# A chain of two transformer blocks on one NeuronCore: instruction order from the detailed timing model, stacked transposes one tile later, V's first step moved, ten products added at the start

## The chip, the cores and the metric

One core of a Trainium2 chip runs the whole program in one launch. The metric is the device time of that launch in microseconds (us), as the median of several executions. One further execution is recorded by the hardware profiler; all rows of the trace come from that one.

## What is computed

Input x has 512 tokens of 1024 features. It goes through two blocks; every intermediate is 32-bit.

```python
def first_block(x, ...):                      # DEPTH = 2
    for i in range(2):
        mix = dsa_mixer(h) if i == 0 else gla_mixer(h)
        h = layer_norm(ALPHA * h + mix)
        h = layer_norm(ALPHA * h + squared_relu_mlp(h, w_up, w_down))
# dsa_mixer: q (16 heads x 64), k, v (4 heads x 64), and an indexer (8 heads x 64) whose scores
#   choose the 128 best keys of each query; softmax attention over the chosen keys; @ w_o
# gla_mixer: gated linear attention with 4 heads; @ w_o
def second_block(x, c, ...):
    mod = silu(c) @ w_ada + b_ada             # six rows: shifts, scales, gates
    h = modulate(rms_norm(x), ...); proj = h @ w_in
    y_attn = axial_gqa_attention(...)         # 8 query heads, 2 key heads, 64 wide, full softmax
    y_mem  = bidirectional_mlstm(...)         # 4 heads x 128
    x = x + g1 * (concat(y_attn, y_mem) @ w_out)
    x = x + g2 * ffn(modulate(rms_norm(x), ...))
    return rms_norm(x)
```

## The kernel before

**Tiling.** Tokens lie in four tiles of 128 rows. The activations stand a second time transposed, split into a high and a low part (`xT_hi`, `xT_lo`) that TensorE multiplies in its faster 32-bit form; each weight piece is split in the same way (`wh`, `wl`, `Net.wsplit`: ScalarE copies the high part at L88, VectorE subtracts at L85). A product of two such operands is three products, high x high, high x low, low x high, all issued by the helper `mm` at L77. That is why most rows of TensorE are on L77.

**Order.** The code is written with a tile scheduler. It simulates the program, and at every moment gives each engine the ready instruction of highest priority, which normally is the one that the program wrote first. The result is a fixed instruction stream per engine; on the chip each engine works its stream in that order and waits where an operand isn't ready. `Net.urgent` gives weight loads and weight splits a priority ahead of everything else. Before the change the simulation behind this is the library's default one.

**Two hand-written lists** say which step the program writes when. `ORDER_A` is for the first block's attention: S is a score tile of the indexer, B the search for the best keys of a tile (16 rounds on VectorE, L533 and L534, closed by L535), V a step of V's projection (two tiles of tokens), Q0 and Q1 steps of the query projections, A an attention tile (tile, head group), O an output projection tile, X the reload of x. `ORDER_2` does the same for the second block (VM, AQ and KV are projections, C the convolution's, A attention, M and N the mLSTM).

**Projections.** `proj_steps` (L146) multiplies tile by tile and calls `evac(t, ps)` when a tile's sum stands in PSUM. For the heads that go into attention, `evac` rotates the tile on VectorE, splits it into high and low parts stacked side by side (`hst`, `kst`, `qst`), and calls `transpose_stack` (L398), which transposes them on TensorE (L405) and copies them out on ScalarE (L407). The buffers `qst` and `kst` of the second block are single.

**Start.** `load_x` (L1412) loads the four token tiles in halves, in the order 1, 2, 3, 0, and between them the first weight chunk; it writes the split of these weights first and the transposes of the tokens (`transpose_half`, L298) after it.

**Big stages.** `w_sums` and `proj_seven` do seven half-size products in place of eight in the MLPs: 44 groups of them, each closed by additions on VectorE (L290 to L294).

Of the kernel before, what the change touches and what calls it, by code (L numbers as in the profile page):

```python
# [11 lines left out]
F32R = mybir.dt.float32r  # L12
# [5 lines left out]

ORDER_A = "S2 V S3 V S1 Q0 B1 Q0 A00 A10 Q1 A11 B2 A20 A01 B3 Q1 A30 X A21 O O O A31 O".split()


ORDER_2 = [x.split() for x in ("VM VM AQ AQ KV W KV C",
# [2 lines left out]
P = 128  # L27
# [10 lines left out]
class Net:  # L38
    def __init__(self, ctx, tc, ins, out):
        self.tc, self.nc, self.ins, self.out = tc, tc.nc, ins, out  # L40
        nc = self.nc
        self.cp = ctx.enter_context(tc.tile_pool(name="cp", bufs=1))
        self.wp = ctx.enter_context(tc.tile_pool(name="wp", bufs=2))
        self.sp = ctx.enter_context(tc.tile_pool(name="sp", bufs=4))
        self.pp = ctx.enter_context(tc.tile_pool(name="pp", bufs=2, space=PSUM))
        self.new_xt()
        self.xh = self.cp.tile([P, KB, S], F32R, name="xT_hi")
        self.xl = self.cp.tile([P, KB, S], F32R, name="xT_lo")
        self.ident = self.cp.tile([P, P], F32, name="ident")
        make_identity(nc, self.ident)  # L50
        self.identr = self.cp.tile([P, P], F32R, name="identr")
        nc.vector.tensor_copy(self.identr, self.ident)
        self.epst = {}
        self.nurgent = 0

    def new_xt(self):
        self.xt = self.cp.tile([P, NT, D], F32, tag="xt", name="x_tok")
# [2 lines left out]
    @contextmanager  # L60
    def urgent(self):

        was = self.tc.cur_priority
        self.tc.cur_priority = start = -1000000 + self.nurgent
        yield
        self.nurgent += self.tc.cur_priority - start
        self.tc.cur_priority = was

    def const(self, val):
        if val not in self.epst:  # L70
# [75 lines left out]
    def proj_steps(self, ah, al, chunks, n, evac, tiles=range(NT), serial=False, tags="a"):  # L146


        tiles = list(tiles)
        nck = len(chunks)  # L150
        got = {}
        for t0 in ([[t] for t in tiles] if serial else [tiles] if nck == 1 else [tiles[i : i + 2] for i in range(0, len(tiles), 2)]):
            ps = {}
            for ci in range(nck):
                if ci not in got:
                    got[ci] = chunks[ci]()
                wh, wl, ks = got[ci]
                for t in t0:
                    if ci == 0:
                        ps[t] = self.bank(tags[t % len(tags)])  # L160
                    ts = slice(t * P, (t + 1) * P)

                    prods = [(x(k)[:, ts], wh[:, j, :]) for j, k in enumerate(ks) for x in (ah, al)]
                    prods += [(ah(k)[:, ts], wl[:, j, :]) for j, k in enumerate(ks)]
                    for i, (x, y) in enumerate(prods):
                        self.mm(ps[t][:, :n], x, y, ci == 0 and i == 0, ci == nck - 1 and i == len(prods) - 1)
                    if ci == nck - 1:
                        evac(t, ps[t][:, :n])
            yield

# [286 lines left out]
def layer_a(net, first):  # L457
    nc, tc, I = net.nc, net.tc, net.ins
    w_in, w_o = I["a_w_in"][0], I["a_w_o"][0]
    xk = net.xk()  # L460
    with tc.tile_pool(name="da", bufs=1) as da:
# [8 lines left out]
        with tc.tile_pool(name="di", bufs=1) as di, tc.tile_pool(name="dr", bufs=2) as dr:  # L470
# [6 lines left out]
            def ev_heads(dst, tofs, h0, scale, pool=False):  # L477
                def f(t, ps):
# [6 lines left out]
                    st = dr.tile([P, 10, 2, 64], F32R, tag="st", name="hst")[:, :8]  # L485
                    split_rot(net, dr, v8, rot, st[:, :, 0, :], st[:, :, 1, :], scale)
                    sv = st.rearrange("p h a d -> p h (a d)")
                    transpose_stack(net, sv, 8, lambda j0, m: dst[:, h0 + j0 : h0 + j0 + m, (t - tofs) * P : (t - tofs + 1) * P])
                return f

            net.proj_tok(*xk, [lambda: (*first, [0, 1, 2, 3]), net.wtok(w_in, (1536, 512))[1]], 512, ev_heads(iqT, 1, 0, None), tiles=range(1, NT))
            def ev_k(t, ps):
# [7 lines left out]
                nc.vector.tensor_copy(st[:, 1, :, 1, :], st[:, 1, :, 0, :])  # L500
                tsl = slice(t * P, (t + 1) * P)
                sv = st.rearrange("p a h b d -> p a h (b d)")
                transpose_stack(net, sv[:, :, 4, :], 2, lambda j0, m: ik[:, :, tsl])
                for a, dst in ((0, kTh), (1, kTl)):
                    transpose_stack(net, sv[:, a], 4, lambda j0, m: dst[:, j0 : j0 + m, tsl])

            net.proj_tok(*xk, net.wtok(w_in, (1024, 256), (2048, 72)), 328, ev_k)

# [48 lines left out]
            for step in ORDER_A:  # L557
                if step in flows:
                    next(flows[step])
                elif step == "X":  # L560
                    reload()
                else:
                    {"S": score, "B": best, "A": attend}[step[0]](*map(int, step[1:]))
        out_ln(net, 0, w_o, have["oa"])

# [439 lines left out]
def second(net):  # L1005
# [5 lines left out]
    with tc.tile_pool(name="sm", bufs=1) as sm:  # L1011
# [8 lines left out]
        with tc.tile_pool(name="sa", bufs=1) as sa:  # L1020
# [27 lines left out]
            with tc.tile_pool(name="sr", bufs=2) as sr:  # L1048
# [27 lines left out]

                def ev_q(t, ps):
                    xn = rope(ps, 8, t, tabs["cq"], tabs["sq"])
                    st = sr.tile([P, 8, 2, 64], F32R, tag="st", name="qst", bufs=1)
                    nc.scalar.activation(st[:, :, 0, :], xn, AF.Copy, scale=-0.125)  # L1080
                    nc.vector.scalar_tensor_tensor(st[:, :, 1, :], xn, -0.125, st[:, :, 0, :].bitcast(F32), op0=ALU.mult, op1=ALU.subtract)
                    transpose_stack(net, st.rearrange("p h a d -> p h (a d)"), 8,
                                    lambda j0, m: qT[:, j0 : j0 + m, t * P : (t + 1) * P])
                flows["AQ"] = net.proj_steps(*xk, net.wtok(w_in, (0, 512)), 512, ev_q)

                def ev_kv(t, ps):
                    xn = rope(ps[:, 0:128], 2, t, tabs["ck"], tabs["sk"])
                    st = sr.tile([P, 2, 2, 2, 64], F32R, tag="st", name="kst", bufs=1)
                    net.split(st[:, 0, :, 0, :], st[:, 1, :, 0, :], xn)
                    nc.scalar.copy(st[:, 0, :, 1, :], st[:, 0, :, 0, :])  # L1090
                    nc.scalar.copy(st[:, 1, :, 1, :], st[:, 1, :, 0, :])
                    tsl = slice(t * P, (t + 1) * P)
                    for i, dst in ((0, kTh), (1, kTl)):
                        transpose_stack(net, st[:, i].rearrange("p h a d -> p h (a d)"), 2,
                                        lambda j0, m: dst[:, j0 : j0 + m, tsl])
                    nc.scalar.activation(v[:, t].rearrange("p g d -> p (g d)"), ps[:, 128:256], AF.Copy)
                    nc.vector.tensor_tensor(gates[:, t, :], ps[:, 256:272], gb, op=ALU.add)  # L1097
                flows["KV"] = net.proj_steps(*xk, net.wtok(w_in, (512, 256), (2816, 16)), 272, ev_kv)
                run_steps(ORDER_2[0][1:], flows, {"W": conv_weights})
            prep = mlstm_prep(net, sm, gates)  # L1100
            with tc.tile_pool(name="sp2", bufs=1) as sp2:
                run_steps(ORDER_2[1], flows, {"A": lambda t: softmax_pv(net, sp2, t, S, NT, qT, kTh, kTl, v, 0, None, oah, oal, 0)})
# [309 lines left out]
def load_x(net, src, w=None):  # L1412

    nc = net.nc
    order = (1, 2, 3, 0)
    n = w.shape[1] if w is not None else 0
    with net.urgent():
        if w is not None:
            raw = net.wp.tile([P, 2048], F32, tag="raw", name="wr")
        for i, t in enumerate(order):  # L1420
            for h in range(2):
                sl = slice(h * 512, h * 512 + 512)
                nc.sync.dma_start(net.xt[:, t, sl], src[t * P : (t + 1) * P, sl])
                if i == 0 and w is not None:
                    for k in (2 * h, 2 * h + 1):
                        nc.sync.dma_start(raw[:, k * n : (k + 1) * n], w[k * P : (k + 1) * P, :])
    if w is not None:
        first = net.wsplit(raw, 4, n, pieces=4)
    for t in order:
        for h in range(2):  # L1430
            net.transpose_half(net.xt[:, t, h * 512 : (h + 1) * 512], net.xh, net.xl, t, h)
    return first if w is not None else None

# [34 lines left out]
STAGES = ["ln1", "mlp1", "ln2", "mlp2", "out"]  # L1468


@with_exitstack
def tile_net(ctx: ExitStack, tc: tile.TileContext, ins, out, first=0, last=4):
    net = Net(ctx, tc, ins, out)
    dp = ctx.enter_context(tc.tile_pool(name="dr_mod", bufs=1, space=bass.MemoryType.DRAM))
    net.mod = dp.tile([6, D], F32, name="mod")
# [47 lines left out]
```

## Time and profile before

| | us |
|---|---|
| median of 3 executions (lowest 1855.94, highest 1859.72) | 1856.32 |
| the profiled execution | 1859.66 |
| its span, first to last instruction | 1857.9 |
| TensorE busy in it | 1815.5 |
| VectorE busy | 1440.5 |
| ScalarE busy | 912.3 |

The span is what the profiler sees of the program; the execution's own time is 1.8 us longer. "Busy" is the union of an engine's instruction times. A matmul's end is modelled and overlaps the next one's start, so its pace is read from the distance between starts. In the rows, PE is TensorE's matmul, PEld its weight load, DVE VectorE, ACT ScalarE; L77 is line 77 of the kernel, and `a<-b,c` is what an instruction writes and reads.

### The profile page before, as it was taken

Reading aid. Unit: us, or ns where it says so; the run is one execution under the profiler, and the core shown is the slowest. Engines: PE = TensorE matmul, PEld = TensorE weight load, DVE = VectorE, ACT = ScalarE, POOL = GpSimd, SP = SyncE. Lnnn points to the kernel's source line nnn. Section 1 sums busy time; section 2 is a strip of 40 time slices with the busy share of each in tenths; the row PEclk is TensorE's granted clock in tenths of the full one; section 3 lists DMA queues with packets and bytes.
Section 4 is the critical chain, followed back from the end, with each engine's and each line's share of the span. In section 5 each row is a group of like instructions: output and inputs, shape, how many; then the busy total and the mean of one; then the engine's idle time right before and its main releaser. Section 6 shows DMA issues by size and latency. Waiting matters only on the chain.

```text
span 1857.9 us, 26802 instructions
## 1 busy us (share of the span) xinstructions
PE 1815.5 (98%) x10564; PEld 1532.8 (83%) x10564; DVE 1440.5 (78%) x2467; ACT 912.3 (49%) x1600; POOL 19.0 (1%) x46
## 2 busy tenths in 40 slices
PE   8999999999999999999999999999999899999997
PEld 7865698988888888889888888777566689999996
DVE  5998589878678587468988777877876787788877
ACT  5568644444443544334544444445677445344334
POOL 0010000000000100000000000000000000000000
PEclk9999999999999999999999999999999999999999
DMA  4231244634324222126454323422112122333232
GB/s 143 91 68 52 67 139 158 207 117 148 103 91 134 61 69 69 68 91 188 140 180 140 113 92 111 139 73 81 46 41 69 45 91 68 114 114 114 79 104 91
DMA packets 127161, 190.80 MB, mean 103 GB/s; under 512 B 9279, under 2 KB 77835, under 8 KB 127036
## 3 DMA queue, kind: packets, MB, share of 16 engines
q1 hardware_dynamic: 126996, 189.03, 32.0%
q8 instruction: 83, 1.36, 0.3%
q14 instruction: 42, 0.34, 0.1%
q0 software_dynamic: 32, 0.07, 0.0%
q10 hardware_dynamic: 8, 0.00, 0.0%
HBM read 186.96 MB, written 2.12 MB: 102 GB/s over the span
## 4 chain that ended last, share of the span: by engine, by line
PE 92%; DVE 5%; ACT 2%; issue 0%; DMA 0%; POOL 0%; SPq 0%; DVEq 0%; ACTq 0%; POOLq 0%
PE ps_a L77 51%; PE ps_s L77 15%; PE ps_t L77 11%; PE ps_o L77 7%; PE ps_t L443 1%; PE ps_t L302 1%; PE ps_s L806 1%; PE ps_a L1275 1%; DVE wl L85 1%; PE ps_t L405 1%; PE ps_s L1241 1%; ACT prob L434 0%; PE ps_s L843 0%; PE ps_o L858 0%; ACT wh L88 0%
## 5 line engine op out<-in xcount | busy, mean ns | idle before, releaser
L88 ACT ACTIVATE wh<-wr 128x1024 fp32r<-128x1024 f32 (+2 forms) x284 | 258.6, 958 | 239.3 <-PE ps_t L77 113.3
L85 DVE TENSOR_TENSOR wl<-wr,wh 128x1024 fp32r<-128x1024 f32 (+2 forms) x284 | 304.1, 1104 | 84.6 <-ACT wh L88 55.1
L77 PE MATMUL ps_a<-wh,xT_hi 128*128 128x512 f32 (+3 forms) x536 | 205.3, 387 | 3.6 <-ACT xT_hi L88 2.2
L77 PE MATMUL ps_a<-wh,xT_lo 128*128 128x512 f32 (+3 forms) x536 | 204.3, 385 | 0.6 <-DVE xT_lo L85 0.6
L88 ACT ACTIVATE wsh<-wr 128x1024 fp32r<-128x1024 f32 x94 | 97.5, 1059 | 184.3 <-DVE wr L254 155.5
L77 PE MATMUL ps_a<-xT_hi,wh 128*128 128x256 f32 (+1 forms) x528 | 163.4, 321 | 0.9 <-DVE gtok L1097 0.5
L77 PE MATMUL ps_a<-xT_lo,wh 128*128 128x256 f32 (+1 forms) x528 | 162.7, 319 | 0.0
L77 PE MATMUL ps_a<-xT_hi,wl 128*128 128x256 f32 (+1 forms) x528 | 147.0, 319 | 0.0
L77 PE MATMUL ps_a<-wl,xT_hi 128*128 128x512 f32 (+3 forms) x536 | 143.6, 381 | 0.0
L77 PE MATMUL ps_s<-wh,hh 128*128 128x512 f32 x344 | 136.6, 397 | 0.1
L77 PE MATMUL ps_s<-wh,hl 128*128 128x512 f32 x344 | 136.7, 397 | 0.0
L77 PE MATMUL ps_a<-tl,wsh 128*128 128x256 f32 x528 | 132.1, 283 | 0.0
L77 PE MATMUL ps_a<-th,wsh 128*128 128x256 f32 x528 | 132.1, 282 | 0.0
L77 PEld LDWEIGHTS ps_a<-wh,xT_hi 128*128 128x128 f32 x536 | 101.5, 189 | 25.0 <-issue 4.5
L85 DVE TENSOR_TENSOR wsl<-wr,wsh 128x1024 fp32r<-128x1024 f32 x94 | 113.0, 1221 | 10.7 <-ACT wsh L88 10.7
L77 PEld LDWEIGHTS ps_a<-wh,xT_lo 128*128 128x128 f32 x536 | 101.5, 189 | 19.8 <-DVE xT_lo L85 1.4
L77 PE MATMUL ps_t<-wh,hl 128*128 128x512 f32 x296 | 117.4, 397 | 0.0
L77 PE MATMUL ps_t<-wh,hh 128*128 128x512 f32 x296 | 117.4, 396 | 0.0
L77 PEld LDWEIGHTS ps_a<-wl,xT_hi 128*128 128x128 f32 x536 | 95.6, 188 | 19.3 <-issue 1.6
L77 PEld LDWEIGHTS ps_a<-xT_hi,wh 128*128 128x128 f32 x528 | 100.1, 190 | 9.3 <-issue 0.8
L77 PEld LDWEIGHTS ps_a<-xT_lo,wh 128*128 128x128 f32 x528 | 100.0, 189 | 7.8 <-issue 0.8
L77 PEld LDWEIGHTS ps_a<-tl,wsh 128*128 128x128 f32 x528 | 100.3, 190 | 0.0
(437 smaller groups left out, 4122.3 us busy)
## 6 DMA issues: line engine op xcount, KB each, us to landing
wr<-in_mlp_w_up_dram SPq DMA_DIRECT2D x32, 1024.0 KB
wr<-in_mlp_w_down_dram SPq DMA_DIRECT2D x32, 1024.0 KB
mod_raw<-in_w_ada_dram SPq DMA_DIRECT2D x48, 512.0 KB
wr<-in_b_w_in_dram SPq DMA_DIRECT2D x12, 1024.0 KB
wr<-in_w_gate_dram SPq DMA_DIRECT2D x11, 1024.0 KB
wr<-in_w_up_dram SPq DMA_DIRECT2D x11, 1024.0 KB
wr<-in_w_in_dram SPq DMA_DIRECT2D x10, 1024.0 KB
wr<-in_w_down_dram SPq DMA_DIRECT2D x10, 1024.0 KB
```

Of the source, the lines that this page charges most:

```text
L77: self.nc.tensor.matmul(ps, lt, rt, start=first, stop=last)
L85: (eng or self.nc.vector).tensor_tensor(out, x, hi.bitcast(F32), op=ALU.subtract)
L88: self.nc.scalar.activation(out, x, AF.Copy)
L302: self.nc.tensor.transpose(ps[:, j * P : (j + 1) * P], src[:, j * P : (j + 1) * P], self.ident)
L405: nc.tensor.transpose(ps[:, j * P : (j + 1) * P], st[:, j0 + j, :], net.identr)
L443: nc.tensor.transpose(pst[:, kb * P : (kb + 1) * P], pr[:, kb * P : (kb + 1) * P], net.ident)
L806: nc.tensor.matmul(ps[:, c * 64 : c * 64 + 64], x[:, c * C : (c + 1) * C], xv[:, c * m : (c + 1) * m, 1, :], start=True, stop=True)
L1241: nc.tensor.matmul(ps, qk[:, 4 + h, a * P : (a + 1) * P], qk[:, h, :], start=True, stop=True)
L1275: nc.tensor.matmul(o, ws[a][:, b * P : (b + 1) * P], v1[:, a, h, 0:129], start=n == 0, stop=n == len(as_) - 1)
```

## The change

- The whole program is put into one block of the scheduler whose simulation is the detailed timing model instead of the default one. Nothing of the computation changes by this, but every engine's order may.
- `transpose_stack` is no longer called in `evac`. It is put on a list (`later`), and the list is worked off (`flush`) when the next tile's products have been written, before a step S, A of `ORDER_A`, and at the end of the second block's projections. `qst` and `kst` get two buffers.
- `ORDER_A` begins with V, S2 in place of S2, V.
- Five products of the identity with itself into a PSUM bank that nothing reads (`warm`) stand behind the making of the identity, and five more behind the transposes of the first loaded half tile. These transposes are written ahead of the first weight chunk's split, with urgent priority.

```diff
-ORDER_A = "S2 V S3 V S1 Q0 B1 Q0 A00 A10 Q1 A11 B2 A20 A01 B3 Q1 A30 X A21 O O O A31 O".split()
+ORDER_A = "V S2 S3 V S1 Q0 B1 Q0 A00 A10 Q1 A11 B2 A20 A01 B3 Q1 A30 X A21 O O O A31 O".split()
...
         make_identity(nc, self.ident)
+        self.warm(5)
...
+    def warm(self, n):
+        with self.urgent():
+            ps = self.bank("s")
+            for _ in range(n):
+                self.nc.tensor.matmul(ps[:, :P], self.ident, self.ident, start=True, stop=True)
...
+    def later(self, f):
+        self.pend.append(f)
+
+    def flush(self):
+        todo, self.pend = self.pend, []
+        for f in todo:
+            f()
...
                     if ci == nck - 1:
+                        self.flush()
                         evac(t, ps[t][:, :n])
...
-                    transpose_stack(net, sv, 8, lambda j0, m: dst[:, h0 + j0 : h0 + j0 + m, (t - tofs) * P : (t - tofs + 1) * P])
+                    net.later(lambda: transpose_stack(net, sv, 8, lambda j0, m: dst[:, h0 + j0 : h0 + j0 + m, (t - tofs) * P : (t - tofs + 1) * P]))
...
-                transpose_stack(net, sv[:, :, 4, :], 2, lambda j0, m: ik[:, :, tsl])
-                for a, dst in ((0, kTh), (1, kTl)):
-                    transpose_stack(net, sv[:, a], 4, lambda j0, m: dst[:, j0 : j0 + m, tsl])
+
+                def turn():
+                    transpose_stack(net, sv[:, :, 4, :], 2, lambda j0, m: ik[:, :, tsl])
+                    for a, dst in ((0, kTh), (1, kTl)):
+                        transpose_stack(net, sv[:, a], 4, lambda j0, m: dst[:, j0 : j0 + m, tsl])
+                net.later(turn)
...
+                    if step[0] != "B":
+                        net.flush()
                     {"S": score, "B": best, "A": attend}[step[0]](*map(int, step[1:]))
...
-                    st = sr.tile([P, 8, 2, 64], F32R, tag="st", name="qst", bufs=1)
+                    st = sr.tile([P, 8, 2, 64], F32R, tag="st", name="qst", bufs=2)
...
                 run_steps(ORDER_2[0][1:], flows, {"W": conv_weights})
+                net.flush()
...
     if w is not None:
+
+        with net.urgent():
+            net.transpose_half(net.xt[:, order[0], 0:512], net.xh, net.xl, order[0], 0)
+        net.warm(5)
         first = net.wsplit(raw, 4, n, pieces=4)
     for t in order:
-        for h in range(2):
+        for h in range(1 if w is not None and t == order[0] else 0, 2):
...
+def tile_net(tc: tile.TileContext, ins, out, first=0, last=4):
+    with tc.block(schedule_with_timeline_sim=True):
+        tile_all(tc, ins, out, first, last)
+
+
 @with_exitstack
-def tile_net(ctx: ExitStack, tc: tile.TileContext, ins, out, first=0, last=4):
+def tile_all(ctx: ExitStack, tc: tile.TileContext, ins, out, first, last):
```

The queries (`qst`) and the keys (`kst`) of the second block are deferred in the same way as the two above.

## Rows read from the trace of the kernel before

**Rows 1.** Part 1 of the page: busy us (share of the span) xinstructions of TensorE.

```profile
PE 1815.5 (98%) x10564; PEld 1532.8 (83%) x10564; DVE 1440.5 (78%) x2467; ACT 912.3 (49%) x1600; POOL 19.0 (1%) x46
```

**Rows 2.** Busy time by stretch: from:to us, length, five engines, PEclk, DMA share, GB/s.

```profile
0.00:17.00 17.00, 10.31 (x46) 7.94 (x47) 7.74 (x17) 8.64 (x13) 1.08 (x8) 1.00 0.83 287
100.00:173.00 73.00, 68.49 (x350) 45.53 (x349) 66.09 (x252) 57.73 (x175) 6.37 (x16) 1.00 0.22 47
173.00:200.00 27.00, 24.73 (x124) 15.29 (x123) 18.71 (x67) 24.04 (x59) 0.00 (x0) 1.00 0.21 79
200.00:1190.00 990.00, 989.17 (x5827) 857.42 (x5826) 757.59 (x1063) 440.33 (x647) 8.63 (x8) 1.00 0.38 121
1190.00:1215.00 25.00, 20.94 (x90) 15.86 (x89) 24.23 (x48) 9.34 (x25) 0.00 (x0) 0.93 0.13 43
1255.00:1285.00 30.00, 27.05 (x149) 21.93 (x147) 19.81 (x64) 21.38 (x51) 0.52 (x1) 0.89 0.25 78
1300.00:1345.00 45.00, 40.48 (x192) 25.54 (x190) 39.92 (x83) 28.82 (x56) 0.00 (x0) 0.96 0.18 48
1440.00:1480.00 40.00, 34.40 (x170) 27.04 (x169) 27.72 (x57) 20.18 (x58) 0.00 (x0) 0.96 0.16 52
1520.00:1840.00 320.00, 320.00 (x2126) 292.66 (x2125) 256.84 (x334) 135.00 (x187) 0.00 (x0) 1.00 0.31 99
```

**Rows 3.** Pieces of the chain that ended last: start us, us, what.

```profile
58.21 2.87 PE ps_a L77 x24
...
372.78 2.80 PE ps_s L77 x12
```

**Rows 4.** Groups of instructions by line: busy us, mean ns | idle before.

```profile
L77 PEld LDWEIGHTS ps_s<-wh,hh 128*128 128x128 f32 x344 | 64.9, 189 | 15.3 <-ACT hh L88 1.2
...
L290 DVE TENSOR_TENSOR eu<-eo,ps_a 128x512 f32<-128x512 f32 x44 | 30.2, 686 | 35.4 <-PE ps_a L77 33.6
```

**Rows 5.** TensorE's waits: us in total, times, longest us.

```profile
PE ps_t L302 <- DVE rows_tl L981: 3.4, 2, 2.7
```

**Rows 6.** Busy time by stretch, behind the wait for the keys.

```profile
1266.00:1273.00 7.00, 6.75 (x20) 5.11 (x21) 3.57 (x24) 3.04 (x11) 0.00 (x0) 0.51 0.77 256
```

**Rows 7.** Instructions in order of time, opening: start us, us, engine, line, what [idle before].

```profile
1.13 0.29 POOL masks.py:199 TENSOR_SCALAR_AFFINE_SELECT ident<-ident 128x128 f32<-128x128 f32 x1
...
3.58 1.09 PE L302 MATMUL ps_t<-ident,x_tok 128*128 128x128 f32 x4 [3.58 <-DMA x_tok<-in_x_dram]
4.23 0.63 ACT L88 ACTIVATE wh<-wr 128x512 fp32r<-128x512 f32 x1 [1.61 <-DMA wr<-in_a_w_in_dram]
...
6.13 1.12 PE L302 MATMUL ps_t<-ident,x_tok 128*128 128x128 f32 x4 [1.46 <-DMA x_tok<-in_x_dram]
...
8.91 0.79 PE L77 MATMUL ps_a<-wh,xT_hi 128*128 128x512 f32 x1 [1.47 <-ACT xT_hi L88]
...
12.51 0.63 PE L77 MATMUL ps_a<-wh,xT_lo 128*128 128x512 f32 x1
...
12.93 0.61 PE L77 MATMUL ps_a<-wh,xT_hi 128*128 128x512 f32 x1
...
15.42 2.00 ACT L88 ACTIVATE wh<-wr 128x1024 fp32r<-128x1024 f32 x2
```

**Rows 8.** Instructions in order of time around the second block's keys.

```profile
1261.19 4.72 DVE L85 TENSOR_TENSOR wl<-wr,wh 128x1024 fp32r<-128x1024 f32 x4 [0.64 <-ACT wh L88]
...
1265.35 0.36 PE L405 MATMUL ps_t<-identr,kst 128*128 128x128 f32 x2 [2.32 <-ACT kst L1090]
...
1266.25 0.79 PE L77 MATMUL ps_a<-xT_hi,wh 128*128 128x512 f32 x1 [0.55 <-DVE gtok L1097]
```

**Rows 9.** Instructions in order of time, first score product and end of the last top-k.

```profile
52.24 0.93 PE L77 MATMUL ps_s<-iq 128*128 128x384 f32 x4
...
172.72 0.42 DVE L535 TENSOR_SCALAR sc<-sc 128x512 f32<-128x512 f32 x1
173.17 0.69 DVE L428 CUSTOM_DVE_ANT_0 prob<-ps_s,sc 128x512 f32<-128x512 f32 x1
```

More of the change, by code (lines that the diff above doesn't have):

```diff
@@ L45, in __init__ @@
         self.pp = ctx.enter_context(tc.tile_pool(name="pp", bufs=2, space=PSUM))
+        self.epst = {}
+        self.pend = []
+        self.nurgent = 0
         self.new_xt()
@@ L50, in __init__ @@
         make_identity(nc, self.ident)
+        self.warm(5)
         self.identr = self.cp.tile([P, P], F32R, name="identr")
         nc.vector.tensor_copy(self.identr, self.ident)
-        self.epst = {}
-        self.nurgent = 0
+    def warm(self, n):
[3 more added lines that the diff above has]
+                self.nc.tensor.matmul(ps[:, :P], self.ident, self.ident, start=True, stop=True)
     def new_xt(self):
@@ L1078, in ev_q @@
                     xn = rope(ps, 8, t, tabs["cq"], tabs["sq"])
-                    st = sr.tile([P, 8, 2, 64], F32R, tag="st", name="qst", bufs=1)
+                    st = sr.tile([P, 8, 2, 64], F32R, tag="st", name="qst", bufs=2)
                     nc.scalar.activation(st[:, :, 0, :], xn, AF.Copy, scale=-0.125)
                     nc.vector.scalar_tensor_tensor(st[:, :, 1, :], xn, -0.125, st[:, :, 0, :].bitcast(F32), op0=ALU.mult, op1=ALU.subtract)
-                    transpose_stack(net, st.rearrange("p h a d -> p h (a d)"), 8,
-                                    lambda j0, m: qT[:, j0 : j0 + m, t * P : (t + 1) * P])
+                    net.later(lambda: transpose_stack(net, st.rearrange("p h a d -> p h (a d)"), 8,
+                                                      lambda j0, m: qT[:, j0 : j0 + m, t * P : (t + 1) * P]))
                 flows["AQ"] = net.proj_steps(*xk, net.wtok(w_in, (0, 512)), 512, ev_q)
@@ L1087, in ev_kv @@
                     xn = rope(ps[:, 0:128], 2, t, tabs["ck"], tabs["sk"])
-                    st = sr.tile([P, 2, 2, 2, 64], F32R, tag="st", name="kst", bufs=1)
+                    st = sr.tile([P, 2, 2, 2, 64], F32R, tag="st", name="kst", bufs=2)
                     net.split(st[:, 0, :, 0, :], st[:, 1, :, 0, :], xn)
@@ L1092, in ev_kv, with turn @@
                     tsl = slice(t * P, (t + 1) * P)
-                    for i, dst in ((0, kTh), (1, kTl)):
-                        transpose_stack(net, st[:, i].rearrange("p h a d -> p h (a d)"), 2,
-                                        lambda j0, m: dst[:, j0 : j0 + m, tsl])
+                    def turn():
+                        for i, dst in ((0, kTh), (1, kTl)):
+                            transpose_stack(net, st[:, i].rearrange("p h a d -> p h (a d)"), 2,
+                                            lambda j0, m: dst[:, j0 : j0 + m, tsl])
+                    net.later(turn)
                     nc.scalar.activation(v[:, t].rearrange("p g d -> p (g d)"), ps[:, 128:256], AF.Copy)
```

## The prediction

> **What bounds the kernel now.** I read the share of busy time first, then busy time by stretch, then the chain that ended last, then TensorE's waits.
>
> TensorE is busy 98% of the span [rows 1]. Cut into stretches [rows 2], its idle time, length minus PE busy, is 6.7 us at the start (0 to 17), 4.5 and 2.3 in the first block's attention (100 to 173, 173 to 200), 0.8 in the 990 us of MLP and gated layer, 4.1 at 1190 to 1215, 3.0 at 1255 to 1285, 4.5 at 1300 to 1345, 5.6 at 1440 to 1480, and none in 1520 to 1840, the last MLP; the 18 us behind it are the tail of additions and stores. So the middle has 25 us of waits, start and tail aside. Between them the chain is one product after the other: twelve products of 512 columns take 2.80 us, 233 ns each [rows 3]. No order shortens these.
>
> The Trainium skill (Perfetto Trace Analysis, Identifying the Most-Contended Engine) holds matmul busy time for a bad measure and weight-load busy time for a good one. Weight loads are busy 83% of this span, and by that rule 17% of 1858 us, 316 us, would be open. The trace does not bear this out: a weight load takes 189 ns [rows 4] of the 233 ns that a product needs in a gapless run [rows 3], 81%, so 83% is what a full TensorE looks like here. The measurement decides, and the sum uses the 25 us.
>
> A second loss is the clock. In four stretches behind waits (1201 to 1205, 1266 to 1273, 1337.7 to 1341.2, 1457 to 1461) the granted clock averages 0.57, 0.51, 0.51 and 0.57 ([rows 6] have the longest; the four rows are alike). Read as time at the lower level, 1.2 GHz, that is 3.4 + 6.9 + 3.4 + 3.4 = 17.1 us, and half of it, 8.6 us, is lost. The opening is a fifth: its clock column has nothing to tell, but products of 512 columns start 0.42 us apart at 12.5 to 12.9 us [rows 7], half the pace of [rows 3].
>
> **The change part by part.** Numbers are against the profiled execution, 1859.7 us (span 1857.9 plus 1.8 around it); the median of the runs shown is 3.3 us lower, 1856.3, and I subtract that at the end.
>
> *Opening (ten unread products, first half tile transposed ahead).* The identity is ready at 1.4 us, the first token half is there at 3.6 and the second at 6.1 [rows 7]. Five products of 128 columns cost no more than the four transposes of the same shape and type, 1.09/4 = 0.27 us each, 1.4 us in all; five fit before 3.6 us and five into the 1.46 us of waiting before 6.1. So they cost nothing on the path; if the tokens came as soon as the identity, they would cost 2.7. What they may give is the clock. What the early transposes give: the split of the first half no longer stands behind four weight pieces. Now the first product starts at 8.91; the half's transposes end at 4.7 and the first weight piece is copied at 4.9 [rows 7], one copy of half a microsecond more makes 5.4. In those 3.5 us, at 0.42, eight products can run. Each was due later, where products run gapless up to 100 us, at 0.23: 1.9 us. The second weight chunk is copied only at 15.4 us [rows 7] and its products can't move. The half-pace stretch, 8.9 to 12.9, is worth at most 2.0 more. I take -2.5, bounds 0 and -4.
>
> *V's first step ahead of score S2.* Four tiles' projection in two steps; a step has two tiles of 24 products of 256 columns, 2.87 us for 24 [rows 3], so 5.7 us. S2's first product now runs at 52.24 [rows 9] and can start up to 5.7 us later. S2 loads nothing and V's weight loads are urgent wherever V stands, so no transfer on SyncE's queue is passed. Behind it on VectorE stand the scores and the three top-k searches; the last one ends at 172.7 and the last attention tile begins right behind it [rows 9]. VectorE is 91% busy in 100 to 173 [rows 2], so this chain sets the stage's end. But 24 of these products now run at 58.21 [rows 3], amid the scores, which are then shorter by as much. I take 0, bounds 0 and +5.7.
>
> *Transposes one tile later.* None is added or removed, and no load goes with them; they only drop behind the next tile's products. They gain what TensorE waits for them, above all 2.32 us for the second tile's keys in the second block, where four weight splits, 4.72 us, stand ahead on VectorE. With 0.55 us for a gate addition behind it [rows 8] 2.9 us are lost there, in a stretch where VectorE is busy 66% [rows 2], so most can be filled. The copies by ScalarE and the scores move back by the next tile's last twelve products (12 x 0.12 to 12 x 0.233, 1.4 to 2.8 us); what covers this is the next flow's products, which need none of the transposed parts. The stacked parts live longer, and the buffers go from one to two where they were single. I take -2, bounds 0 and -3.
>
> *Order by the detailed model.* This renews the queue of every engine, DMA issue included. Where it can gain: 6.8 us of waits in 100 to 200, 4.5 in 1300 to 1345 and 5.6 in 1440 to 1480. An in-order queue that waits with other work behind it is what a better forecast removes, but VectorE is 91%, 89% and 69% busy there [rows 2], and in 1190 to 1215 it is 97% busy: the 3.4 us of waiting for its modulated halves [rows 5] stay. For the others I take a quarter to a third, -2, -1.5 and -1.5; bounds nothing and all, -16.9.
>
> *Clock.* If those waits shrink, so do the half-speed stretches. The longest follows the keys' wait, 2.32 plus 0.55 us; without the wait it would give back 3.4. In 100 to 200, 6.8 us of smaller waits left the clock at 1.00 [rows 2], so the tie is loose. I take -2, bounds 0 and -8.6. By the Trainium skill (TensorE: Matmul & The Clock Gate, Part 1) half speed is the default and activity lifts it; taken strictly, all four go with their waits. By it this term is -8.6.
>
> *New waits.* The 1,310 us without gaps can only lose. The nearest row is the 0.8 us of idle time in 990 us [rows 2]; below nothing it can't go by more than that. I take +2 for all of it, bounds -0.8 and +18 (rival below). The block's entry is one jump per engine; nothing in the trace shows it, I take 0, bounds 0 and the 1.8 us that the execution now has around its span.
>
> Sum: -2.5 + 0 - 2 - 5 - 2 + 2 = -9.5 us. 1859.7 - 9.5 = 1850.2 for an execution like the profiled one, and 1846.8 for a median.
>
> **The rivals.** *The waits only change places.* VectorE is the second bound in both attention stages, so a filled hole on TensorE comes back as a wait for the same VectorE result. For it: 89 to 97% busy; against it: 66 and 69% in the two other stretches. Then the opening's 2.5 stays, less a microsecond or two of V: 1855.
>
> *New waits in the gapless stages, slower.* The new order puts a weight split ahead of a group's combining additions, or the reverse, at each of the 44 seven-product groups [rows 4], as it stands at 1261 us, where four splits hold back a small step. With 0.4 us per group (a third of one split, 4.72/4 = 1.18 us) it costs 44 x 0.4 = 17.6: 1846.8 + 17.6 = 1864. It decides from 9.5/44 = 0.22 us per group. Against it: 0.8 us of waits in 990 us now, and TensorE is never short of ready products there; for it, VectorE is 77% busy with the same two kinds of work.
>
> *All clock stretches go with their waits.* Each of the four begins behind a wait of TensorE ([rows 5, 8] have two of these); if the new order fills them, 8.6 us come back in place of 2: another 6.6, 1840. Against it: it asks that the wait for the modulated halves go too, which hangs on a 97% busy VectorE. (This is what the Trainium skill's Part 1, named above, comes to here.)
>
> *The order hardly differs* where TensorE is gapless and the attention stage's end hangs on the top-k: then opening and keys alone, -4.5: 1852.
>
> **How the numbers follow.** The forecast has 0.42, the clock rival 0.09, the small gain of 1852 0.12, places changed 0.14, new waits 0.23. Under 0.2% (3.7 us, about what a measurement of this kernel can tell) either way is "same": 1852.6 to 1860. The forecast, the clock rival and about three quarters of the 1852 case are faster: 0.60. Places changed and the rest make 0.17. Slower 0.23. The range reaches from 1835, the forecast with all clock stretches and half of the attention waits gone, to 1864, the slower rival.
>
> **What would show it.** In the profile after: first product near 5.4 us and half pace ended before 12.9; no wait on the stacked keys near 1262 and no low clock behind it; PE idle in 100 to 200 nearer 5 than 6.8; the last top-k step no later than 173; still under 1 us of idle between the attention stage and 1190. The forecast is wrong if TensorE's busy time grows, if waits appear in the seven-product groups, or if the last top-k step comes later than 175.

## The result and the profile after

| | us |
|---|---|
| before, median of 4 executions | 1858.0 |
| after, median of 4 executions | 1944.8 |
| ratio, 95% interval | 1.046 (1.044 to 1.049) |
| the profiled execution after, its span | 1945.7, 1943.9 |

The change costs 4.6%; the forecast was a gain of half a percent. Part 1 of the page after, to be read against [rows 1]:

```profile
PE 1843.7 (95%) x10584; PEld 1557.3 (80%) x10584; DVE 1441.3 (74%) x2467; ACT 915.2 (47%) x1605; POOL 19.6 (1%) x46
```

The span grew by 86.0 us. VectorE and ScalarE do the same work as before, within 3 us. TensorE's busy time grew by 28.2 us. Only the ten products of the opening were added (two records each, so the count grows by 20); they take about 4.6 us of it, as the rows of the opening show further down. The rest of the span's growth, 57.8 us, is idle time of TensorE (span less busy: 42.4 before, 100.2 after). So two losses: waits, and products that run slower; the mean granted clock of the span fell from 0.993 to 0.973.

Busy time by stretch after (columns as in [rows 2]):

```profile
50.00:100.00 50.00, 50.00 (x296) 43.56 (x294) 35.90 (x85) 29.41 (x59) 0.00 (x0) 1.00 0.36 99
100.00:125.00 25.00, 21.52 (x105) 17.62 (x103) 24.28 (x66) 13.21 (x29) 5.17 (x12) 0.95 0.29 60
125.00:150.00 25.00, 12.29 (x34) 6.91 (x33) 24.64 (x88) 5.50 (x22) 0.00 (x0) 0.64 0.19 42
150.00:175.00 25.00, 16.64 (x81) 11.45 (x81) 15.61 (x66) 15.38 (x49) 1.80 (x4) 0.80 0.00 1
175.00:200.00 25.00, 22.99 (x112) 13.67 (x111) 15.36 (x74) 22.39 (x75) 0.00 (x0) 1.00 0.00 1
300.00:600.00 300.00, 300.00 (x1869) 267.80 (x1868) 241.11 (x291) 136.19 (x178) 0.00 (x0) 1.00 0.43 139
1240.00:1270.00 30.00, 23.98 (x91) 18.82 (x90) 28.88 (x56) 9.27 (x23) 0.00 (x0) 0.83 0.27 93
1520.00:1600.00 80.00, 68.64 (x378) 59.27 (x377) 56.60 (x102) 30.30 (x72) 0.00 (x0) 0.89 0.13 40
```

The long seven-product stretch, 300 to 600, is still without a gap at full clock. The loss stands in the first block's attention (26.6 us of TensorE idle in 100 to 200, against 6.8 before) and at later stage borders. Where TensorE waits for long, the clock column falls: 0.64 in 125 to 150. Smaller waits can leave it alone: in 175 to 200 it stays at 1.00 beside 2.0 us of idle time. The first stretch has a second sign: VectorE is busy 35.9 of 50 us, in the same stretch before it was 47.1:

```profile
50.00:100.00 50.00, 50.00 (x292) 42.70 (x291) 47.09 (x123) 28.78 (x58) 0.00 (x0) 1.00 0.33 99
```

TensorE's waits after (columns as in [rows 5]):

```profile
PE ps_s L95 <- DVE mn L447: 20.7, 12, 15.1
PE ps_t L321 <- DVE xT_lo L103: 10.6, 5, 5.3
PE ps_s L95 <- ACT prob L453: 7.0, 12, 1.4
PE ps_a L95 <- DVE xT_lo L103: 6.0, 4, 2.4
PE ps_t L321 <- DVE rows_tl L1005: 5.3, 1, 5.3
```

The longest, 15.1 us, and what VectorE does until it ends (instructions in order of time; L557 closes a search, and its width tells whose it is: 256 is tile 1, 384 tile 2, 512 tile 3):

```profile
130.15 0.34 DVE L557 TENSOR_SCALAR sc<-sc 128x384 f32<-128x384 f32 x1
...
149.02 0.42 DVE L555 MAX8 m<-sc 128x8 f32<-128x256 f32 x1
149.35 0.41 DVE L557 TENSOR_SCALAR sc<-sc 128x512 f32<-128x512 f32 x1
...
150.19 0.43 DVE L555 MAX8 m<-sc 128x8 f32<-128x256 f32 x1
150.65 0.09 DVE L556 MATCH_VALUE_LOAD sc<-m,sc 128x8 f32 x1
...
155.10 0.29 DVE L557 TENSOR_SCALAR sc<-sc 128x256 f32<-128x256 f32 x1
155.43 0.42 DVE L447 CUSTOM_DVE_ANT_0 prob<-ps_s,sc 128x256 f32<-128x256 f32 x1
...
155.92 0.58 PE L95 MATMUL ps_s<-kTh,qT 128*128 128x256 f32 x1 [15.09 <-DVE mn L447]
```

Before, the searches closed in the order of their use, and the first masked attention stood right behind the first:

```profile
110.09 0.28 DVE L535 TENSOR_SCALAR sc<-sc 128x256 f32<-128x256 f32 x1
...
114.96 0.40 DVE L428 CUSTOM_DVE_ANT_0 prob<-ps_s,sc 128x256 f32<-128x256 f32 x1
...
124.29 0.34 DVE L535 TENSOR_SCALAR sc<-sc 128x384 f32<-128x384 f32 x1
```

The last was tile 3's at 172.7 [rows 9]. After, tile 1's search, the shortest and the first to be used, closes last, and the masked attention starts 40 us later (155.4 against 115.0). The last search as such ends earlier than before, 155 against 173: that sign, which I had named as one to look for, came true in a kernel that lost 87 us.

### The profile page after: what moved, and what is told of

Its sections match the earlier page's. It is cut to its first block, busy times and chain, and to the rows that moved or that the text cites. A ratio compares the mean times of both kernels' runs of the same rounds, so it can differ in the third digit from the quotient of the medians.

```text
span 1943.9 us, 26773 instructions
## 1 busy us (share of the span) xinstructions
PE 1843.7 (95%) x10584; PEld 1557.3 (80%) x10584; DVE 1441.3 (74%) x2467; ACT 915.2 (47%) x1605; POOL 19.6 (1%) x46
## 4 chain that ended last, share of the span: by engine, by line
PE 84%; DVE 10%; ACT 4%; issue 1%; DMA 0%; SPq 0%; POOL 0%; POOLq 0%; DVEq 0%; ACTq 0%
PE ps_a L95 47%; PE ps_s L95 13%; PE ps_t L95 11%; PE ps_o L95 6%; DVE wl L103 2%; PE ps_s L830 1%; PE ps_a L1303 1%; ACT prob L453 1%; PE ps_t L321 1%; PE ps_t L462 1%; DVE x_tok L345 1%; PE ps_s L1269 1%; PE ps_t L424 1%; DVE sc L556 1%; DVE mn L450 1%
## 5 line engine op out<-in xcount | busy, mean ns | idle before, releaser
L95 PEld LDWEIGHTS ps_a<-th,wsh 128*128 128x128 f32 x528 | 100.3, 190 | 1.6 <-ACT wsh L106 0.5
```

The costliest lines, as they stand in the source:

```text
L95: self.nc.tensor.matmul(ps, lt, rt, start=first, stop=last)
```

## The experiments

A ratio is to the kernel before, measured beside each run, with its 95% interval.

**Which edit it is.** First, all edits without the block; the block alone; the block with the default simulation; the opening alone.

```diff
-    with tc.block(schedule_with_timeline_sim=True):
-        tile_all(tc, ins, out, first, last)
+    tile_all(tc, ins, out, first, last)
```

> All edits of the change except the block with the detailed timing model: the order comes from the library's default simulation again. Theory A (the order made by the detailed model costs the 87 us): 1848 to 1856 us, with the gains of the opening and of the keys' transposes left over. Rival B (the transposes one tile later, and V ahead, cost it, by making queries and keys late for the first attention): 1920 us or more. If both share it, between 1870 and 1920.

> The kernel before, and only the block with the detailed timing model added. Theory A: 1930 to 1955 us, with waits of TensorE at the stage borders and a long wait for VectorE near 140 us as in the changed kernel. Rival B: 1845 to 1860 us.

> The changed kernel with the same block around the whole program, but with the default simulation in it. Theory A: as without a block, 1848 to 1856 us. Rival C (the block itself costs it, by its entry or by what it makes the scheduler hold back at its border): 1930 us or more.

| run | median us | ratio |
|---|---|---|
| all edits, no block | 1862.7 | 1.001 (1.000 to 1.002) |
| block with the detailed model alone | 1953.5 | 1.050 (1.049 to 1.052) |
| all edits, block with the default simulation | 1863.1 | 1.002 (1.001 to 1.003) |

Theory A holds, B and C fall: the detailed model's order alone costs 94 us (1953.5 less 1859.3 of before beside it), the block as such nothing that shows (the two intervals without the detailed model overlap). But theory A's own 1848 to 1856 for these two runs was missed by 7 us: without the detailed order the other edits gain nothing, they cost 2 to 4 us.

**The other edits one by one**, under the default order. The opening (the lines of `warm` and of `load_x` in the change's diff):

> The kernel before, and only the opening's edits: the ten unread products and the first half tile's transposes ahead of the first weight split. By the forecast's first term 2.5 us less than before (0 to 4): 1854 to 1858, with the first weight product near 5.4 us. In the changed kernel the first weight product starts at 9.64 us, later than the 8.91 of before; if the edit itself does that, the time here is 0 to 2 us above before.

It came out at 1.0011 (1.0002 to 1.0021), some 2 us slower, the other way than the forecast's term. The first weight product starts at 11.39 us, not at 5.4. Instructions in order of time:

```profile
1.47 2.50 PE L62 MATMUL ps_s<-ident 128*128 128x128 f32 x10 [1.47 <-POOL ident masks.py:199]
3.76 1.06 PE L310 MATMUL ps_t<-ident,x_tok 128*128 128x128 f32 x4
...
7.34 1.30 ACT L96 ACTIVATE wh<-wr 128x512 fp32r<-128x512 f32 x2 [0.97 <-DMA wr<-in_a_w_in_dram]
...
8.54 1.07 ACT L96 ACTIVATE xT_hi<-ps_t 128x512 fp32r<-128x512 f32 x2
...
10.15 1.11 PE L310 MATMUL ps_t<-ident,x_tok 128*128 128x128 f32 x4 [2.81 <-DVE xT_lo L93]
...
11.39 0.80 PE L85 MATMUL ps_a<-wh,xT_hi 128*128 128x512 f32 x1
```

The five unread products stand as ten records and hold TensorE from 1.47 to 3.76 us, 0.46 us each; the prediction had 0.27. The first transposes, which ran at 3.58 before [rows 7], come at 3.76. ScalarE's copy of them still stands behind all four weight pieces, and the first product behind a third group of transposes that waits 2.81 us until VectorE has read the first group out of PSUM. In the changed kernel all ten products stand ahead of the first transposes, which then start at 5.90.

The transposes one tile later (the lines with `later` and `flush`, and the buffers from one to two):

> The kernel before, and only the stacked parts' transposes one tile later (with the two-fold buffers), default order. By the forecast's second term 2 us less (0 to 3), the 2.3 us wait for the second block's keys and the low clock behind it gone: 1854 to 1859. Rival (the waits change places): the keys' wait is gone, another of the same size stands in the second block's projections or attention, 1858 to 1862.

0.9995 (0.9986 to 1.0004), 1857.4 us: no difference. The keys' wait and the low clock behind it are gone, and a new idle stretch stands in the attention behind (busy time by stretch; [rows 2] have 0.89 in the first of these, and before TensorE was busy 55.00 of 55 us in the second):

```profile
1255.00:1285.00 30.00, 30.00 (x170) 24.78 (x169) 23.44 (x64) 23.45 (x52) 0.52 (x1) 1.00 0.35 113
...
1345.00:1400.00 55.00, 47.70 (x212) 26.95 (x212) 38.35 (x78) 35.01 (x64) 0.00 (x0) 1.00 0.11 42
```

V's first step ahead:

```diff
-ORDER_A = "S2 V S3 V S1 Q0 ...
+ORDER_A = "V S2 S3 V S1 Q0 ...
```

> The kernel before (default order), and only V's first step ahead of score S2. By the forecast's term 0, bounds 0 to +5.7 us: 1857 to 1863. The kernel with all edits but the block is 2 to 4 us above before and has a new wait of 5.9 us of the attention's scores for VectorE; if V's step is its cause, this run has that wait and is 2 us or more above before; if it is the opening (2.5 us alone) or the later transposes (0 alone), it has not.

1.0020 (1.0011 to 1.0029), 3.7 us slower. The scores start 6 us later and end 2 us later (ScalarE's copies of them run from 59 to 80 us, before from 53 to 78), so they were shortened as forecast. But VectorE idles meanwhile (42.27 us busy in 50 to 100, 47.09 before), the last search closes at 176.98 against 172.72, and the wait of 5.99 us that the expectation asked for is there:

```profile
178.19 0.80 PE L77 MATMUL ps_s<-kTh,qT 128*128 128x512 f32 x1 [5.99 <-DVE mn L428]
```

**Where the order loses.** The kernel before was cut into two blocks behind the first attention layer, and the detailed model given either part.

```diff
+    with tc.block(schedule_with_timeline_sim=X):
         fw = load_x(...)
+        layer_a(net, fw)
+    with tc.block(schedule_with_timeline_sim=Y):
+        (the stages behind it)
```

> The kernel before, cut into two blocks behind the first block's attention layer, both ordered by the default simulation. It measures the cut itself: nothing that stands behind it, such as the next stage's weight loads, can be issued ahead of it. 1862 to 1880 us by every theory; the next two runs are read against it.

> The same cut, and the detailed model orders the part ahead of it (opening and first attention layer), the default simulation the rest. Theory A1 (the detailed order loses where chains of dependent steps have independent products beside them, the first attention layer above all): 35 to 45 us above the cut kernel with the default order, as that stage ends 38 us later in the changed kernel's trace. Rival (the loss is spread evenly over the program): 10 to 15 us, the stage's share of the time.

> The same cut, and the detailed model orders only the part behind it. Theory A1: 45 to 55 us above the cut kernel with the default order, with the waits at the borders of the stages (layer norms, gated layer, mLSTM) and none in the long seven-product stretches. Rival (spread evenly): 75 to 85 us.

The cut alone gives 1870.1 us, the detailed order ahead of it 1904.7 (34.7 more), behind it 1926.0 (55.9 more). The sum, 90.6, is about what the whole block costs. The first attention layer with the opening is an eighth of the time and carries 38% of the loss: it is not spread evenly. Both figures lie within 1 us of theory A1's ranges and far from the rival's.

**What happens in the first attention layer.** The indexer's scores in the changed kernel (instructions of TensorE; each row of `iq` is one head's pair):

```profile
66.50 0.52 PE L95 MATMUL ps_s<-iq 128*128 128x384 f32 x2
...
67.80 0.51 PE L95 MATMUL ps_s<-iq 128*128 128x384 f32 x2
...
71.89 0.51 PE L95 MATMUL ps_s<-iq 128*128 128x384 f32 x2
...
73.17 0.51 PE L95 MATMUL ps_s<-iq 128*128 128x384 f32 x2
```

Two heads, then sixteen other products before the next: 5.4 us for two heads, of which VectorE needs 1.2. Are the heads held by their two PSUM banks, or paced by VectorE?

```diff
-                    ps = net.bank("s")
+                    ps = net.bank("st"[h % 2])
```

> The changed kernel, and the indexer's scores use four PSUM banks in turn (the two of the tag s and the two of t) in place of two. In the changed kernel two heads' scores run and then 16 to 20 other products, 5.3 us for two heads. Theory D (the detailed model commits TensorE's next products some 20 ahead, before a score's bank is free, so that a score that becomes ready goes behind them): twice as many heads in each round trip, the three score tiles end near 90 to 100 us in place of 119, and the whole is 10 to 25 us faster than the changed kernel's 1945. Rival E (the model holds VectorE's steps for longer than they are, and the scores are paced by these): the banks don't matter, 1940 to 1950 us.

1943.8 us, 1.0446 (1.043 to 1.046): the time of the changed kernel, so the gain that theory D asked for is not there. Its sign for the scores is: four heads now share a round trip.

```profile
77.18 0.62 PE L95 MATMUL ps_t<-iq 128*128 128x512 f32 x2
77.64 0.63 PE L95 MATMUL ps_s<-iq 128*128 128x512 f32 x2
78.80 0.63 PE L95 MATMUL ps_t<-iq 128*128 128x512 f32 x2
79.27 0.63 PE L95 MATMUL ps_s<-iq 128*128 128x512 f32 x2
82.77 0.63 PE L95 MATMUL ps_t<-iq 128*128 128x512 f32 x2
```

In this order a head whose bank comes free goes behind some sixteen products that already stand on TensorE's queue. The scores' last step on VectorE came at 108 in place of 123 us, but the searches still ended at 155, and the wait behind them was 16.0 us. So I forced the searches' order, and, for the borders, the layer norms' one by one.

```diff
+                if t - 1 in bias and t > 1:
+                    nc.vector.scalar_tensor_tensor(sc[:, 0:1], bias[t - 1][:, 0:1], 0.0, sc[:, 0:1], op0=ALU.mult, op1=ALU.add)
                 for rnd in range(16):
```

> The changed kernel, and the three searches for the best keys made to run one after the other in the written order (tile 1, 2, 3): the first element of a tile's scores takes a term of zero from the search before. In the changed kernel they end in the order tile 2 (130 us), 3 (149), 1 (155), because their rounds are taken in turn, and every attention tile with a search mask starts behind 155, against 115 before. Theory T (the detailed order takes the steps of several chains in turn, so that the chain needed first ends last): tile 1 ends near 130, the masked attention starts there, and 15 to 25 us of the changed kernel's 1945 go. Rival R (the attention stage is late because its independent products were spent early, 98 to 119 us, and nothing is left to fill with): the start moves, the end of the stage does not, 1938 to 1947 us.

```diff
-        mv = sp.tile([P, 2], F32, name="mv")
-        sd = sp.tile([P, 1], F32, name="sd")
-        rs = sp.tile([P, 1], F32, name="rs")
+        v4 = sp.tile([P, 4], F32, name="lnv", bufs=1)
+        mv, sd, rs = v4[:, 0:2], v4[:, 2:3], v4[:, 3:4]
```

> The changed kernel, and the layer norm's small values (mean, deviation, its inverse) in one single buffer, so that a tile's normalisation ends before the next tile's begins. In the changed kernel tiles 0 and 1 are normalised in step, and TensorE waits 10.6 + 6.0 us for the low parts of the new activations at the borders of the stages. Theory T: the first tile is ready 3 to 4 us earlier at each of the four borders, 6 to 15 us of 1945 go. Rival R2 (the border waits come from the weight splits that stand ahead on VectorE): less than 4 us, and the waits stay.

> Both of the two edits above together. Theory T: the sum of the two, 1905 to 1925 us. If both act on one and the same wait, no better than the better of the two.

All three miss theory T: 1948.4, 1946.8 and 1950.1 us (1.0475, 1.0476, 1.0492). The rivals are nearer. With serial layer norms no time is gained; the waits for `xT_lo` fall from 16.6 to 9.5 us in all, but a new one of 6.8 us, for which the profile shows no cause, stands at a transpose. With serial searches, tile 1's closes at 140.65 and the masked attention starts there, but tile 3's closes at 206.41, 57 us later than in the changed kernel (149.35), because nobody may begin it earlier, and the wait has moved:

```profile
206.41 0.43 DVE L559 TENSOR_SCALAR sc<-sc 128x512 f32<-128x512 f32 x1
...
207.63 0.79 PE L95 MATMUL ps_s<-kTh,qT 128*128 128x512 f32 x1 [7.62 <-DVE mn L447]
```

The remedy held VectorE idle: in 100 to 125 us it is busy 14.5 of 25 us, in the changed kernel 24.3. The next pair lets the first search start first without holding any back, by the list alone.

```diff
-ORDER_A = "V S2 S3 V S1 Q0 ...
+ORDER_A = "V S1 S2 V S3 Q0 ...
```

> The changed kernel, with the score tiles written in the order 1, 2, 3 (V S1 S2 V S3 in place of V S2 S3 V S1), so that the search that the attention needs first also starts first, and nothing holds VectorE back from the other searches' rounds as the serial run did. Theory T2 (the stage is late because the first search ends last, 155 against 110 us, and the serial run gave its 14 us back only because its added dependence kept VectorE idle until 118): the masked attention starts 20 us or more earlier and 15 to 30 us of the changed kernel's 1945 go. Rival R (the stage's end hangs on VectorE's whole work and on products spent early, whatever search is first): 1938 to 1948 us.

> The run before and the four banks for the scores together. Theory T2: the scores no longer hold VectorE up either, 20 to 35 us less than 1945. Rival R: 1936 to 1948 us. If the four banks help only where the search order is mended, the difference to the run before is 5 us or more; the four banks alone gave none.

> The kernel before (default order), with the score tiles written in the order 1, 2, 3 (S1 V S2 V S3). Control for the two runs above: if the list itself is the better one, it gains here too. There the searches already end in the order 1, 2, 3 (110, 124, 173 us), so by both theories 1854 to 1862 us.

Under the detailed order 1930.6 us, 1.0384 (1.037 to 1.040), some 14 us less than the changed kernel; with four banks 1933.9, no better. Closings and first masked attention of the former:

```profile
105.04 0.28 DVE L557 TENSOR_SCALAR sc<-sc 128x256 f32<-128x256 f32 x1
...
127.98 0.40 DVE L447 CUSTOM_DVE_ANT_0 prob<-ps_s,sc 128x256 f32<-128x256 f32 x1
...
146.56 0.34 DVE L557 TENSOR_SCALAR sc<-sc 128x384 f32<-128x384 f32 x1
...
161.25 0.42 DVE L557 TENSOR_SCALAR sc<-sc 128x512 f32<-128x512 f32 x1
```

So rival R falls. T2's masked attention is there, 27 us earlier, but its gain is just under the 15 to 30. The four banks qualify what the first closing means:

```profile
132.78 0.28 DVE L557 TENSOR_SCALAR sc<-sc 128x256 f32<-128x256 f32 x1
...
134.10 0.41 DVE L447 CUSTOM_DVE_ANT_0 prob<-ps_s,sc 128x256 f32<-128x256 f32 x1
```

With them tile 1's search closes 28 us later than in the run without, the masked attention starts only 6 us later, and the time is 3 us longer. In the run without, TensorE's score products of tile 0, which needs no search, run until 123.6 us, 18 us behind that closing: there the search was no longer what the masked attention waited for.

The control is the kernel before with the scores in that order and V where it had stood, behind the first of them:

```diff
-ORDER_A = "S2 V S3 V S1 Q0 ...
+ORDER_A = "S1 V S2 V S3 Q0 ...
```

It wasn't neutral: under the default order it gives 1855.2 us, 0.9970 (0.9958 to 0.9982), **0.3% faster than the kernel before**. There tile 1's search closes at 89.40 instead of 110.09, and the masked attention starts at 108.89 instead of 114.96. Of the 14 us some 5 (0.30% of 1860) are therefore the list's own, as far as the two lists, which differ in V's place, can be set against each other; by this estimate about 9 are mended order.

**A faster kernel, and the borders.**

The control's list and the later transposes together, under the default order:

> The kernel before (default order) with the two edits that did not lose: the score tiles in the order 1, 2, 3 (0.997 of before alone) and the stacked parts' transposes one tile later (0.9995 alone). If they add up, 0.996 to 0.997, 1852 to 1855 us where before is 1858 to 1860. If they share a wait, or the later transposes give back in the second block's attention what they gain at its keys, 0.997 to 0.999.

0.9986 (0.9977 to 0.9995): the two edits don't add up. The list alone has the lowest ratio, though the two intervals overlap. Then the borders. At the first layer norm of the changed kernel (instructions in order of time):

```profile
284.43 1.22 DVE L103 TENSOR_TENSOR wl<-wr,wh 128x1024 fp32r<-128x1024 f32 x1
...
286.24 2.35 DVE L103 TENSOR_TENSOR wl<-wr,wh 128x1024 fp32r<-128x1024 f32 x2
288.51 1.28 DVE L103 TENSOR_TENSOR xT_lo<-ps_t,xT_hi 128x512 fp32r<-128x512 f32 x2
...
289.25 1.11 PE L321 MATMUL ps_t<-ident,x_tok 128*128 128x128 f32 x4 [5.28 <-DVE xT_lo L103]
```

Three weight splits, 3.6 us, stand ahead of the parts that TensorE waits for. Before, the same transposes ran at 237 us without a wait, with later tiles' products still there to fill.

```diff
-    def wsplit(self, raw, kb, n, name="w", pieces=2):
+    def wsplit(self, raw, kb, n, name="w", pieces=4):
```

> The changed kernel, with each weight chunk split in four pieces in place of two. In TensorE's waits over 0.9 us at the borders of the stages of the changed kernel, VectorE works 13 us on weight splits of 1.2 us each. Theory B (a fixed number of steps is committed ahead on VectorE, so that smaller splits hold up what follows for a shorter time): 4 to 9 us less than 1945, and the waits for xT_lo shorter. Rival (all splits that are ready are taken ahead, whatever their size): 1942 to 1955, as each piece costs 0.1 us of its own.

1951.8 us, 1.0504 (1.049 to 1.052): slower. Theory B falls: the waits of the transposes for `xT_lo` grew from 10.6 to 16.6 us, and the smaller pieces only cost more.

## Why the prediction was wrong

*What bounds the kernel*: right that the gapless stretches had nothing to gain, wrong that they had almost nothing to lose. The long seven-product stretch kept its 300.00 of 300 us. But the 990 us with 0.8 us of idle time also hold stage borders, and in the changed kernel 19.6 us of idle time stand between the attention stage and the second block; I had named "under 1 us" as the sign to look for:

```profile
262.00:1240.00 978.00, 958.36 (x5633) 835.31 (x5632) 730.34 (x1005) 428.97 (x612) 8.60 (x8) 0.99 0.37 119
```

The reading that a full TensorE has its weight loads 81 to 83% busy was too low as well: in the two gapless stretches of [rows 2] they are busy 87% and 91%.

*Order by the detailed model*, the term of -5 with bounds of nothing and -16.9: this step failed. It asked only which holes a better forecast could fill, and excluded a loss, though every engine's order was to be made anew and the order before already kept TensorE 98% busy. Alone it measures +94. The reasoning was that a more detailed model makes a better order. In its place the runs show an order that, in the first attention layer, takes the steps of the three searches in turn, so that the first one used closes last and TensorE waits 15.1 us; 34.7 us are lost there and 55.9 behind it. Half of this was in the prediction: the searches as the chain that sets the stage's end, on a VectorE that is 91% busy. I read only their last end. The runs say that the start of the masked attention counts too, as long as the later searches keep up: with the scores in the order 1, 2, 3 it starts 27 us earlier and the time falls by 14 us, although the last search closes 6 us later; with serial searches it starts 14 us earlier, the last search closes 51 us later than any in the changed kernel, and nothing is gained.

*New waits*, +2 with an upper bound of 18: the right kind of loss, priced in the wrong place. I put it at the 44 seven-product groups; the stretches of these that are shown stayed whole. Weight splits did come ahead of what TensorE waited for, but at the stage borders, 5.3 us a time at the worst, where few independent products are left.

*Clock*, -2: wrong in its sign. The term assumed that waits would go; new ones came. With the block alone, which adds no product, TensorE's busy time is 1841.4 us, 25.9 more than before; that it would grow was one of my signs of a wrong forecast. The tie of clock and waits held at the keys: in the run with later transposes alone their wait went, and the clock of that stretch is 1.00 in place of 0.89. But it is loose, as the prediction said: in the same run the 7.3 us of idle time in 1345 to 1400 left the clock at 1.00. The Trainium skill (TensorE: Matmul & The Clock Gate, Part 1) has half speed as the default, lifted by activity; the 0.89 that became 1.00 agrees with it.

*Opening*, -2.5: wrong at "one copy of half a microsecond more makes 5.4"; the first product came at 11.39 us alone and at 9.64 in the changed kernel. ScalarE works its stream in order, and the stream still had four weight pieces ahead of that copy. The price of the unread products was wrong too: they were taken as cheap as transposes, 0.27 us, and cost 0.46 us each, so five don't fit before the first tokens. Alone the opening costs 2 us.

*V's first step*, 0 with bounds to +5.7: 3.7, within the bounds. The cover that I named was there for the scores, 6 us later at their start and 2 at their end; but VectorE's loss meanwhile is not made good, and the last search ends 4.3 us later. These 4.3 us, and not the 2 by which the scores end later, are near the 3.7 that it cost.

*Transposes one tile later*, -2: the named wait went and 7.3 us of idle time came in 1345 to 1400; the sum is zero. That is the rival "the waits only change places", at this one edit.

*Block entry*, 0: right within 2 us (1.002 against 1.001). No row shows what the entry consists of.

The slower rival at 1864 had the right side, but its 17.6 us of new waits are a fifth of the 94 us that the order alone costs. What stays open: of the 35 us in the first attention layer about 9 are, by the estimate above, the order of scores and searches; that the rest is VectorE's early idling together with products spent too early is argued from the traces, not shown. Of the 56 us behind it no single cause was isolated; serial layer norms and smaller splits both missed. And the other edits gain 7 us when the block is there (1.050 against 1.046) but none without it; by which of them was not tried.

## What to carry to other kernels

An order that keeps the main engine 98% busy is an asset: a change that makes all of it anew has a large downside, and the bounds must say so, whatever the new planner is called. In a static order look at which of several parallel chains is used first and when its use can begin, and not only at the last end; a remedy that starts the first one earlier by holding the others back gained nothing here. Before hiding a wait, ask what the same engine will do behind it: the later transposes removed the wait they named and gave it back in the next stage.

## What the runs showed of the hardware

Three things were not expected. In the searches VectorE starts an independent instruction some 0.09 us before the former's recorded end (the close at 149.35 against 149.02 + 0.42), a dependent one 0.03 us behind it (150.65 against 150.19 + 0.43). Over the searches of the changed kernel the median of this gap is -0.081 us where two run in turn (135 to 149 us) and +0.034 where one runs alone (150 to 155). Taking two in turn thus saves about 0.11 us (an estimate, the difference of the two medians) at each step that would wait for the one before it. At this point the detailed order saves time, and it lost on the whole; that the model chose it for this reason is not shown. (The Trainium skill, VectorE: DVE Perf Modes, The DRAIN you can't avoid, has a chain of copies that takes the same time with a semaphore after each and with only one at the end. No run here repeats that test; the rows here set apart whether an instruction needs the one before it.)

The second is the price of a product in plain 32-bit form. Each unread product stands as two records, 0.21 us apart at the lower clock level: 0.43 us for 128 columns, as much as a product of the split form needs at that level for 512 (0.42 [rows 7]).

The third is that the unread products did raise the clock, but it didn't last. In the run of the opening alone their records stand 0.21 us apart until 5.3 us and 0.11 us apart from 5.5 us on, and in the changed kernel the second group of transposes, at 6.90 us, takes 0.66 us in place of 1.12 [rows 7]. Then (busy time by stretch, opening of the changed kernel):

```profile
6.50:9.90 3.40, 1.32 (x9) 0.80 (x7) 2.14 (x5) 2.11 (x5) 0.00 (x0) 1.00 1.00 333
9.90:13.40 3.50, 3.16 (x10) 2.52 (x10) 1.81 (x3) 0.77 (x2) 0.00 (x0) 0.51 1.05 402
```

TensorE was busy 1.3 of the 3.4 us in the first row, waiting for the split of the tokens, and the first weight products then ran at half speed: from 11.84 to 12.69 us they start 0.43 us apart.
